# A decoder trunk in split fp32 on one core: seams of its squared-ReLU layers rearranged

## The chip, the core and the metric

The kernel runs on one core of a Trainium2 chip. A core has five engines that work side by side and each run their own instructions in order: TensorE (PE: matmuls and transposes into PSUM), VectorE (DVE), ScalarE (ACT), GpSimd (POOL) and SyncE (SP), which here issues the DMAs. They meet through semaphores. The metric is the device time of one execution in microseconds (us); before the change it is 2891.88 us, the median of three runs (2891.14 to 2891.97).

## What is computed

The reference is a trunk of two layers over 1024 tokens of width 1024 in fp32. Each layer has three sub-layers, all of the form h + RMSNorm(f(RMSNorm(h))) with a gain on both norms: a token mixer, a cross-attention into 256 memory tokens, and a squared-ReLU MLP. The mixer of layer 0 is a matrix-memory and recurrent block, that of layer 1 a sliding-window attention with rotary positions.

```python
def rms_norm(x, g):
    xf = x.astype(jnp.float32)
    y = xf * lax.rsqrt(jnp.mean(xf * xf, axis=-1, keepdims=True) + EPS)
    return (y * g.astype(jnp.float32)).astype(x.dtype)

def squared_relu_mlp(u, w1, w2):          # w1: 1024 x 4096, w2: 4096 x 1024
    return jnp.square(jax.nn.relu(u @ w1)) @ w2

    for l in range(DEPTH):                # DEPTH = 2
        u = rms_norm(h, g_mix_pre[l])
        # layer 0: mlstm_rglru_mixer(u, ...), layer 1: sliding_window_sink_attention(u, ...)
        h = h + rms_norm(u, g_mix_post[l])
        u = memory_cross_attention(rms_norm(h, g_x_pre[l]), mem, g_mem[l], w_xq[l], w_xkv[l], w_xo[l])
        h = h + rms_norm(u, g_x_post[l])
        u = squared_relu_mlp(rms_norm(h, g_ff_pre[l]), w_ff1[l], w_ff2[l])
        h = h + rms_norm(u, g_ff_post[l])
```

## The kernel before

Every fp32 operand of a product is split into a high and a low part (names ending in `h` and `l`: `split`, ScalarE copies the high part, VectorE subtracts for the low one), and a product is three matmuls of 128 x 128 by 128 x 512 on TensorE (`mm3`). Tokens are worked on in eight tiles of 128; tiles 0 to 3 and 4 to 7 are the two halves. A row of h stands in SBUF tiles of 128 x 1024, two column halves of 512.

The MLP is computed by the Strassen-Winograd scheme, seven products in place of eight, for both of its matrix products. In the first product the column blocks of `w1` run in 16 steps (the loop `for i in range(NP)`, with products p1 to p7 in each) and the squared result goes to DRAM (`hid`). In the second product the sum over 4096 runs in four chunks c, and each chunk has seven products in the order of the table `order`: p = 1, 2, 6, 5, 3, 7, 4. I call one of these 28 products a job; a job has four tiles of 128 tokens, each of 12 matmuls. Its left operand (`sh`) is loaded from `hid` in two halves `ar` by `lefts` and split; its right operand comes from four 1 MB blocks `b` of `w2` per chunk (`load_block`, `block_of`). The results stand in PSUM tiles `pa` and `pb` and are summed up by VectorE into the `acc` tiles (`gather`, and `tt`, an elementwise add or subtract). The pair 2 goes on in the PSUM tiles of 1, 3 in those of 5, 4 in those of 7. Where a bank `pb` is asked for, three tiles come from one PSUM pool (`G`) and the fourth from another (`T`), which also gives the tiles of the transposes (`tr`) and of the squares (`junk`).

After the last chunk comes the post-norm with the residual: `post(t)` for each tile adds the `u` part, squares it (ScalarE, with a sum along the row), multiplies it by the gain (GpSimd, `post_half`), takes the inverse root of the sum (`rsqrt`, a start value and three Newton steps on 128 x 1 numbers, nine small VectorE instructions), loads h, multiplies and adds (`post_norm`), and stores. In layer 0 the next mixer's pre-norm follows for the first four tiles (`pre_norm`): squares, root, `un` = h times root, then transposes on TensorE, which VectorE multiplies by the gain (`ut`) and ScalarE and GpSimd split into `uh` and `ul` (`transposed`). For the MLP's input the second half of the tokens goes through `transposed_sum`, which also forms Winograd's sums of the two halves.

The order of each engine's instructions is set by the code: `defer(delay, fn)` puts a piece of work into a queue that is emptied as a modelled clock of TensorE (`pe(us)`) passes its due time. `UD` is the delay from `un` to the transposes for the MLP's input, `MD` that for the next mixer's input, `N1` that from the squares to the root. `ready(u)` runs the queue until all tiles of an operand are there. TensorE's order is exactly the order of the code; the Tile framework orders the others.

## Time and profile before

| what | value |
|---|---|
| median of three runs | 2891.88 us |
| profiled execution | 2894.48 us |
| its span, first to last instruction | 2892.7 us |
| TensorE busy | 2686.7 us (93%) |
| VectorE busy | 2047.8 us (71%) |
| ScalarE busy | 1387.8 us (48%) |
| GpSimd busy | 546.9 us (19%) |
| mean granted clock of TensorE | 0.960 of full speed |

The times of all engines lie beside each other, so only the busy share of the fullest one says how near the program is to its bound; what an engine waited for, and where, is told by the list of waits and by the timeline. In them each row names the line of the kernel, the operation, its output and inputs, and in brackets the idle time before it with what ended that idle time. An `x` number says how many like instructions a row joins.

### The profile page before, as it was taken

How to read it: one execution, taken by the hardware profiler on the slowest of the kernel's cores; microseconds unless marked ns; L12 is line 12 of the kernel's file. 1: busy time of each engine (PE TensorE's matmuls, PEld its weight loads, DVE VectorE, ACT ScalarE, POOL GpSimd, SP SyncE). 2: the span in 40 equal slices, each digit the busy share in tenths (PEclk: the TensorE clock that was granted, in tenths of full speed). 3: DMA queues.
4: the chain of work that ended last, by engine and by line, in shares of the span. 5: the costliest groups of instructions: out<-in, count | busy, mean ns of one | idle time of the engine just before them, and what ended most of it. 6: DMA issues, size and time to landing. Idle time of an engine off the chain costs nothing. (4 is left out here: it accounts for less than half of the span.)

```text
span 2892.7 us, 35705 instructions
## 1 busy us (share of the span) xinstructions
PE 2686.7 (93%) x12846; PEld 2221.4 (77%) x12846; DVE 2047.8 (71%) x3604; ACT 1387.8 (48%) x2535; POOL 546.9 (19%) x434
## 2 busy tenths in 40 slices
PE   8999999999979999899987889879997999989996
PEld 8878778778867888788865668757886888878885
DVE  7776586656767666667786985785676766666778
ACT  5555545436544544443343773663544544444332
POOL 1351243442120000000023451560212000000003
PEclk9999999899999999999988989989998999999998
DMA  8633542225413444744334154023442344474433
GB/s 253 195 91 99 177 139 77 84 95 167 154 70 130 145 148 153 273 156 145 122 110 138 37 182 153 23 73 113 162 141 91 121 156 142 146 282 147 153 117 117
DMA packets 297314, 395.97 MB, mean 137 GB/s; under 512 B 16712, under 2 KB 172848, under 8 KB 297136
## 3 DMA queue, kind: packets, MB, share of 16 engines
q1 hardware_dynamic: 297136, 393.68, 41.2%
q8 instruction: 101, 1.65, 0.2%
q14 instruction: 77, 0.63, 0.1%
HBM read 297.15 MB, written 96.47 MB: 136 GB/s over the span
## 5 line engine op out<-in xcount | busy, mean ns | idle before, releaser
L230 DVE TENSOR_TENSOR w<-wr,w 128x1024 fp32r<-128x1024 f32 x248 | 321.0, 1297 | 208.8 <-ACT w L229 207.8
L83 PE MATMUL g<-uh,w 128*128 128x512 f32 x1152 | 378.5, 399 | 0.0
L83 PE MATMUL pa<-t,sh 128*128 128x512 f32 x1536 | 356.1, 392 | 17.4 <-ACT sh L229 16.8
L83 PEld LDWEIGHTS pa<-t,sh 128*128 128x128 f32 x1536 | 290.8, 190 | 80.1 <-ACT sh L229 17.7
L229 ACT ACTIVATE w<-wr 128x1024 fp32r<-128x1024 f32 x248 | 261.2, 1055 | 102.8 <-DMA wr<-in_w_xkv 26.6
L385 POOL TENSOR_TENSOR acc<-acc,gain 128x512 f32<-128x512 f32 x32 | 44.7, 1417 | 1262.0 <-DMA gain<-in_g_ff_post 1188.3
L83 PE MATMUL pb<-t,sh 128*128 128x512 f32 x1152 | 266.5, 392 | 3.0 <-DVE acc L767 3.0
L83 PEld LDWEIGHTS pb<-t,sh 128*128 128x128 f32 x1152 | 217.8, 189 | 48.8 <-DVE acc L767 3.5
L83 PEld LDWEIGHTS g<-uh,w 128*128 128x128 f32 x1152 | 217.2, 189 | 49.4
L229 ACT ACTIVATE t<-b 128x2048 fp32r<-128x2048 f32 x56 | 107.5, 1923 | 299.8 <-PE pa L83 164.5
L83 PE MATMUL g<-ul,w 128*128 128x512 f32 x576 | 228.4, 396 | 1.5 <-POOL ul L321 1.5
L230 DVE TENSOR_TENSOR sh<-ar,sh 128x1024 fp32r<-128x1024 f32 x112 | 136.8, 1234 | 100.7 <-PE pa L83 51.6
L83 PE MATMUL b<-t,w 128*128 128x512 f32 x768 | 180.0, 390 | 0.0
L321 POOL TENSOR_TENSOR ul<-ut,uh 128x512 fp32r<-128x512 f32 x80 | 114.2, 1449 | 345.8 <-ACT uh L320 345.8
L83 PE MATMUL g<-w,uh 128*128 128x512 f32 (+1 forms) x640 | 172.2, 359 | 3.4 <-ACT g L1464 3.4
L83 PE MATMUL b<-uh,wa 128*128 128x512 f32 x512 | 171.7, 396 | 1.5 <-ACT pc L847 1.5
L83 PEld LDWEIGHTS b<-t,w 128*128 128x128 f32 x768 | 144.2, 188 | 31.1
L83 PE MATMUL g<-w,pTh 128*128 128x512 f32 x512 | 160.1, 394 | 0.5 <-ACT pTh L229 0.5
L230 DVE TENSOR_TENSOR t<-b,t 128x2048 fp32r<-128x2048 f32 x56 | 127.8, 2285 | 2.1 <-ACT t L229 2.1
L83 PEld LDWEIGHTS g<-ul,w 128*128 128x128 f32 x576 | 108.8, 189 | 25.1 <-POOL ul L321 1.8
L83 PEld LDWEIGHTS g<-w,uh 128*128 128x128 f32 x640 | 110.1, 191 | 18.1 <-ACT g L1464 3.8
L83 PEld LDWEIGHTS b<-uh,wa 128*128 128x128 f32 x512 | 96.2, 188 | 25.4 <-ACT pc L847 2.3
(391 smaller groups left out, 5923.6 us busy)
## 6 DMA issues: line engine op xcount, KB each, us to landing
ar<-hid SPq DMA_DIRECT2D x112, 512.0 KB, 4.0
h<-h SPq DMA_DIRECT2D x100, 512.0 KB, 3.6
b<-in_w_ff SPq DMA_DIRECT2D x36, 1024.0 KB, 5.1
wr<-in_w_ff SPq DMA_DIRECT2D x64, 512.0 KB, 3.9
hid<-s SPq DMA_DIRECT2D x128, 256.0 KB, 2.3
wr<-in_ev_w_in SPq DMA_DIRECT2D x48, 512.0 KB, 3.8
hid<-c SPq DMA_DIRECT2D x94, 256.0 KB, 2.0
wr<-in_w_xkv SPq DMA_DIRECT2D x32, 512.0 KB, 5.9
```

The costliest lines, as they stand in the source:

```text
L83: ins = nc.tensor.matmul(*ar, **kw)
L229: act(out=h, in_=src, func=AF.Copy)
L230: (eng or vec).tensor_tensor(out=l, in0=src, in1=f(h), op=ALU.subtract)
L321: pool.tensor_tensor(out=ul[:, q], in0=t, in1=f(uh[:, q]), op=ALU.subtract)
L385: eng.tensor_tensor(out=dst, in0=y, in1=g[:, c], op=ALU.mult)
```

## The change

Four things are altered.

First, the transposes of the MLP's second input half are put off by `UL` = 7 units of the modelled clock after `un`, where it was `UD` = 14; those of the next mixer's first half by `MD` = 11, where it was 13.

Second, `lefts` is cut into the loads (`lefts_raw`) and the splits. Job 0's left operand takes both of its halves from the pool `wr`, and job 1's is loaded right behind it, before p6 of the last step of the first product.

Third, the post-norm of the MLP's output is spread over the last chunk. The gain is loaded in job p = 2, and the square and gain of a finished column half are done there (`weigh`), in p = 3, 7 and 4; the `u` part is added to 12, 22 and 21 in p = 6. Roots, residual and store are made for two tiles at once (`post_pair`, `rsqrt2`), at four places in p = 7 and p = 4. For tiles 0 to 3 of layer 0 `post_pair` also makes the next pre-norm up to `un`, which is written over the `acc` tiles.

Fourth, `left` is a set of tiles, and the sliding-window mixer waits for each tile of its operand where it uses it.

```diff
 RATIO = (0.0, 0.0)
-UD, MD = 14.0, 13.0
+UD, UL, MD = 14.0, 7.0, 11.0
 SD, SG = 14.5, 9.5
...
+    def rsqrt2(ss, n):
+        v = small(8, n)
+        x, xh, y, t = v[:, 0:2], v[:, 2:4], v[:, 4:6], v[:, 6:8]
+        vec.scalar_tensor_tensor(out=x, in0=ss[:, :, 0], scalar=D * EPS, in1=ss[:, :, 1], op0=ALU.add, op1=ALU.add)
+        vec.tensor_scalar(
+            out=y.bitcast(I32), in0=x.bitcast(I32), scalar1=-0.5, scalar2=float(0x5F3759DF + (5 << 23)), op0=ALU.mult, op1=ALU.add
+        )
+        vec.tensor_scalar(out=xh, in0=x, scalar1=-0.5 / D, scalar2=None, op0=ALU.mult)
+        for _ in range(3):
+            vec.tensor_tensor(out=t, in0=y, in1=y, op=ALU.mult)
+            vec.tensor_tensor(out=t, in0=t, in1=xh, op=ALU.mult)
+            vec.scalar_tensor_tensor(out=y, in0=t, scalar=1.5, in1=y, op0=ALU.add, op1=ALU.mult)
+        return y
     def gain(ap, in_w=False):
...
                 transposed_sum(un, g, u, first, c)
-            left[id(u)] -= 1
+            left[id(u)].discard(t)
...
         u = (U(n="uh", key=key), U(n="ul", key=key))
-        left[id(u)] = TPH
+        left[id(u)] = set(range(TPH))
         return u
-    def ready(u):
+    def ready(u, t=None):
-        while left[id(u)]:
+        while left[id(u)] if t is None else t in left[id(u)]:
             clock[0] = max(clock[0], pend[0][0])
...
-        def lefts(c, x):
-            h, lo = (wp.tile([P, 4, HALF], F32R, tag="w", name=nm("sh"), bufs=NW) for _ in range(2))
+        def lefts_raw(c, x, home="wh"):
+            rs = []
             for j in range(2):
-                if j == 0:
+                if home[j] == "w":
                     r = wp.tile([P, 2, HALF], F32, tag="wr", name=nm("ar"), bufs=NWR)
...
                 nc.sync.dma_start(out=r, in_=hid[x, r0 : r0 + 2 * P, :].rearrange("(i q) t -> q i t", q=P))
+                rs.append(r)
+            return rs
+        def lefts(rs):
+            h, lo = (wp.tile([P, 4, HALF], F32R, tag="w", name=nm("sh"), bufs=NW) for _ in range(2))
+            for j, r in enumerate(rs):
                 split(h[:, 2 * j : 2 * j + 2], lo[:, 2 * j : 2 * j + 2], r)
...
             if i == NP - 1:
-                left = lefts(0, 0)
+                left = lefts(lefts_raw(0, 0, "ww"))
+                next_raw = lefts_raw(0, 1)
             p6(i)
...
-        def post(t):
...
+        def weigh(key, t):
+            g, n = 4 * (key in ("21", "22")) + t, int(key in ("12", "22"))
+            post_half(acc[key, t], acc[key, t], late["g"], late["sy"][:, 2 * g : 2 * g + 2], n, pool)
+        def post_pair(t0):
+            keys = ("11", "12") if t0 < 4 else ("21", "22")
+            r = rsqrt2(late["sy"][:, 2 * t0 : 2 * t0 + 4].rearrange("p (t n) -> p t n", t=2), "rs")
+            hs = []
+            for j in range(2):
+                t = t0 + j
+                h = load_h(hsrc, t)
+                for n in range(2):
+                    cols = slice(n * HALF, (n + 1) * HALF)
+                    vec.scalar_tensor_tensor(
+                        out=h[:, cols], in0=acc[keys[n], t % 4], scalar=r[:, j : j + 1], in1=h[:, cols], op0=ALU.mult, op1=ALU.add
+                    )
+                    if after is None:
+                        nc.sync.dma_start(out=hdst[t * P : (t + 1) * P, cols], in_=h[:, cols])
+                if after is not None:
+                    nc.sync.dma_start(out=hdst[t * P : (t + 1) * P, :], in_=h)
+                hs.append(h)
+            if after is not None and t0 < 4:
+                ss = small(4, "ss")
+                for j in range(2):
+                    for n in range(2):
+                        square_sum(hs[j][:, n * HALF : (n + 1) * HALF], ss[:, 2 * j + n : 2 * j + n + 1])
+                r = rsqrt2(ss.rearrange("p (t n) -> p t n", t=2), "rs")
+                for j in range(2):
+                    un = [acc[k, t0 + j] for k in keys]
+                    act(out=un[0], in_=hs[j][:, 0:HALF], func=AF.Copy, scale=r[:, j : j + 1])
+                    vec.tensor_scalar(out=un[1], in0=hs[j][:, HALF:D], scalar1=r[:, j : j + 1], scalar2=None, op0=ALU.mult)
+                    after(t0 + j, un)
...
                     rt = block_of(*jobs[n + 1][:2])
-                    left = lefts(jobs[n + 1][0], jobs[n + 1][2])
+                    left = lefts(next_raw if n == 0 else lefts_raw(jobs[n + 1][0], jobs[n + 1][2]))
+                if c == 3 and p == 2:
+                    if t == 0:
+                        late["g"] = gain(a["g_ff_post"][l], True)
+                        late["sy"] = small(16, "sy", 1)
+                    weigh("11", t)
+                if c == 3 and p == 6:
+                    for k2 in ("12", "22", "21"):
+                        tt(acc[k2, t], acc[k2, t], acc["u", t], add)
+                if c == 3 and p == 3:
+                    weigh("12", t)
                 if last and p == 7:
...
                         xpool[0] = "xt"
-                        late["g"] = gain(a["g_ff_post"][l], True)
-                        late["sy"] = small(16, "sy", 1)
-                    else:
-                        post(t - 1)
-                elif last:
-                    post(3 if t == 0 else t + 3)
+                        post_pair(0)
+                    elif t == 1:
+                        post_pair(2)
+                if last:
+                    weigh(key, t)
+                    if p == 4 and t % 2 == 1:
+                        post_pair(t + 3)
             if c < 3:
...
                     load_block(c + 1, 3, 2)
-        post(7)
         if after is None:
...
         for t in range(TPH):
+            ready(u, t)
             ps = proj_tok(ws, u, t)
...
         un = {}
-        ready(uA)
+        if l == 0:
+            ready(uA)
         wpool[0] = WP[l]
...
                 in_steps(rope_tables(), 3, 3.5)
-            cross(l, half, ux[half], hm, hxr, lambda t, h, u=u, first=uf[0] if half else None: pre_norm(h, gf, u, t, UD, "x", first), None if half else mid)
+            cross(l, half, ux[half], hm, hxr, lambda t, h, u=u, first=uf[0] if half else None: pre_norm(h, gf, u, t, UL if first else UD, "x", first), None if half else mid)
         if stop == 2 + 3 * l:
...
                     un["a"] = new_u()
-                if t < TPH:
-                    pre_norm(h, gn, un["a"], t, MD)
+                u = un["a"]
+                c = slice(t * P, (t + 1) * P)
+                def rest():
+                    transposed(h, [(gn, u[0][:, :, c], u[1][:, :, c])])
+                    left[id(u)].discard(t)
+                defer(MD, rest)
```

Three places show how this moves instructions. The first is TensorE at the input of layer 0's MLP, where `tr` are transposes, `b` products of the MLP's first steps, `un_8168` (before) and `un_8189` (after) halves of tile 7's `un`. Before:

```order
2629 L83 MATMUL b_8187<-ul_5578,wa_8182 128x512
2630 L83 MATMUL b_8187<-uh_5577,wa_8182 128x512
2631 L87 MATMUL tr_8200<-cst,un_8035 128x128 x4
2632 L87 MATMUL tr_8207<-cst,un_8036 128x128 x4
2633 L87 MATMUL tr_8221<-cst,un_8112 128x128 x4
2634 L87 MATMUL tr_8228<-cst,un_8113 128x128 x4
2635 L87 MATMUL tr_8242<-cst,un_8168 128x128 x4
2636 L87 MATMUL tr_8249<-cst,un_8169 128x128 x4
2637 L83 MATMUL b_8292<-uh_7058,w_8268 128x512
```

After:

```order
2628 L87 MATMUL tr_8212<-cst,un_8112 128x128 x4
2629 L87 MATMUL tr_8219<-cst,un_8113 128x128 x4
2630 L83 MATMUL b_8208<-uh_5577,wa_8203 128x512
2631 L83 MATMUL b_8208<-ul_5578,wa_8203 128x512
2632 L83 MATMUL b_8208<-uh_5577,wa_8203 128x512 x2
2633 L83 MATMUL b_8208<-ul_5578,wa_8203 128x512
2634 L83 MATMUL b_8208<-uh_5577,wa_8203 128x512 x2
2635 L83 MATMUL b_8208<-ul_5578,wa_8203 128x512
2636 L83 MATMUL b_8208<-uh_5577,wa_8203 128x512
2637 L87 MATMUL tr_8242<-cst,un_8189 128x128 x4
2638 L87 MATMUL tr_8249<-cst,un_8190 128x128 x4
2639 L83 MATMUL b_8292<-uh_7058,w_8268 128x512
```

Before, six of the eight groups of four transposes stand together; now the last tile's two groups are alone, and the four others stand further ahead.

The second is the queue of SP where the MLP's second product begins. Of the loads `ar` before, 10656 is the second half of job 1's left operand and 10728 that of job 2's, and 10798 the first half of job 3's. Before:

```order
413 L980 DMA ar_10798<-hid 128x2x512
414 L838 DMA hid<-c_10535 128x512
415 L965 DMA b_10608<-in_w_ff 128x4x512
416 L965 DMA b_10610<-in_w_ff 128x4x512
417 L965 DMA b_10611<-in_w_ff 128x4x512
418 L965 DMA b_10609<-in_w_ff 128x4x512
419 L838 DMA hid<-c_10554 128x512
420 L838 DMA hid<-s_10620 128x512
421 L838 DMA hid<-s_10619 128x512 x2
422 L838 DMA hid<-s_10620 128x512
423 L980 DMA ar_10656<-hid 128x2x512
424 L980 DMA ar_10728<-hid 128x2x512
```

After, where 10570 is the second half of job 1's left operand, 10722 and 10796 are the first halves of jobs 2 and 3, and 10724 the second half of job 2's:

```order
410 L995 DMA ar_10570<-hid 128x2x512
411 L1008 DMA b_10520<-in_w_ff 128x4x512
412 L853 DMA hid<-c_10517 128x512
413 L995 DMA ar_10722<-hid 128x2x512
414 L995 DMA ar_10796<-hid 128x2x512
...
418 L980 DMA b_10613<-in_w_ff 128x4x512
419 L853 DMA hid<-c_10554 128x512
420 L853 DMA hid<-s_10624 128x512
421 L853 DMA hid<-c_10535 128x512
422 L853 DMA hid<-s_10623 128x512 x2
423 L853 DMA hid<-s_10624 128x512
424 L995 DMA ar_10724<-hid 128x2x512
```

Job 1's second half now stands before the four loads of `b`, job 2's still behind them.

The third is TensorE at the end of layer 0's MLP, where `pb` are tiles of p = 4 and `g` those of the mixer's projection. Before:

```order
5008 L83 MATMUL pb_12470<-t_12485,sh_12488 128x512
5009 L83 MATMUL pb_12470<-t_12484,sh_12489 128x512
5010 L87 MATMUL tr_12864<-cst,un_12633 128x128 x4
5011 L87 MATMUL tr_12873<-cst,un_12633 128x128 x4
5012 L87 MATMUL tr_12882<-cst,un_12686 128x128 x4
5013 L87 MATMUL tr_12891<-cst,un_12686 128x128 x4
5014 L87 MATMUL tr_12900<-cst,un_12735 128x128 x4
5015 L87 MATMUL tr_12909<-cst,un_12735 128x128 x4
5016 L87 MATMUL tr_12918<-cst,un_12784 128x128 x4
5017 L87 MATMUL tr_12927<-cst,un_12784 128x128 x4
5018 L83 MATMUL g_12964<-w_12946,uh_12543 128x512 x2
```

After:

```order
4978 L83 MATMUL pb_12507<-t_12523,sh_12532 128x512
4979 L87 MATMUL tr_12714<-cst,acc_10714 128x128 x4
4980 L87 MATMUL tr_12723<-cst,acc_10938 128x128 x4
4981 L87 MATMUL tr_12732<-cst,acc_10744 128x128 x4
4982 L87 MATMUL tr_12741<-cst,acc_10966 128x128 x4
4983 L83 MATMUL pb_12507<-t_12523,sh_12531 128x512
4984 L83 MATMUL pb_12507<-t_12524,sh_12531 128x512
4985 L83 MATMUL pb_12507<-t_12523,sh_12532 128x512
4986 L87 MATMUL tr_12753<-cst,acc_10758 128x128 x4
4987 L87 MATMUL tr_12762<-cst,acc_10980 128x128 x4
4988 L87 MATMUL tr_12771<-cst,acc_10772 128x128 x4
4989 L87 MATMUL tr_12780<-cst,acc_10994 128x128 x4
```

Before, the eight groups of transposes follow the last matmul of p = 4; now they stand within its second tile, and its last matmul is followed by the projection's first.

## Rows read from the trace of the kernel before

**Rows 1.** The page, engines: busy us (share of the span), instructions.

```profile
PE 2686.7 (93%) x12846; PEld 2221.4 (77%) x12846; DVE 2047.8 (71%) x3604; ACT 1387.8 (48%) x2535; POOL 546.9 (19%) x434
```

**Rows 2.** List of TensorE's waits: us in total, times, longest us.

```profile
PE b L83 <- ACT uh L344: 26.6, 2, 13.3
...
PE tr L87 <- DVE ut L317: 19.0, 4, 15.4
PE pa L83 <- ACT sh L229: 16.8, 2, 8.7
PE tr L87 <- ACT un L304: 11.6, 4, 8.0
```

**Rows 3.** Windows: per engine busy us (instructions), granted clock, DMA share, GB/s.

```profile
1150.00:1200.00 50.00, 46.66 (x204) 37.83 (x202) 33.15 (x35) 24.92 (x32) 0.00 (x0) 0.99 0.69 243
...
1500.00:1550.00 50.00, 17.17 (x59) 13.25 (x60) 40.54 (x108) 18.62 (x41) 19.03 (x15) 0.56 0.59 200
1550.00:1600.00 50.00, 49.23 (x244) 40.30 (x243) 30.31 (x75) 21.47 (x56) 17.66 (x23) 1.00 0.23 72
```

**Rows 4.** Timeline of TensorE at A: start, us, instruction [idle before <-releaser].

```profile
848.38 1.91 PE L87 MATMUL tr<-cst,un 128*128 128x128 f32 x16
...
866.37 0.79 PE L83 MATMUL b<-uh,w 128*128 128x512 f32 x1 [13.30 <-ACT uh L344]
```

**Rows 5.** Timeline of VectorE at A.

```profile
865.23 0.68 DVE L767 TENSOR_TENSOR wr<-wr,wr 128x512 f32<-128x512 f32 x1
865.83 2.29 DVE L230 TENSOR_TENSOR w<-wr,w 128x1024 fp32r<-128x1024 f32 x1
```

**Rows 6.** Timeline of TensorE at B.

```profile
1204.82 1.22 PE L83 MATMUL pa<-t,sh 128*128 128x512 f32 x2 [8.16 <-ACT sh L229]
```

**Rows 7.** Timelines of ScalarE and of SP's queue at B.

```profile
1203.71 1.06 ACT L229 ACTIVATE sh<-ar 128x1024 fp32r<-128x1024 f32 x1 [1.29 <-DMA ar<-hid]
...
1184.25 2.72 SPq L965 DMA_DIRECT2D b<-in_w_ff  x4
...
1192.99 10.22 SPq L980 DMA_DIRECT2D ar<-hid  x5
```

**Rows 8.** Timeline of TensorE at C.

```profile
1477.97 19.20 PE L83 MATMUL pb<-t,sh 128*128 128x512 f32 x84
1500.21 5.49 PE L83 MATMUL pb<-t,sh 128*128 128x512 f32 x12 [3.05 <-DVE acc L767]
1512.59 1.97 PE L87 MATMUL tr<-cst,un 128*128 128x128 f32 x8 [6.89 <-ACT junk L295]
...
1543.63 2.79 PE L87 MATMUL tr<-cst,un 128*128 128x128 f32 x12 [15.37 <-DVE ut L317]
1546.08 1.14 PE L83 MATMUL g<-w,uh 128*128 128x512 f32 x2
```

**Rows 9.** Timeline of VectorE at C.

```profile
1513.64 1.11 DVE L284 SCALAR_TENSOR_TENSOR rs<-rs 128x1 f32<-128x1 f32 x1
...
1528.08 0.22 DVE L284 SCALAR_TENSOR_TENSOR rs<-rs 128x1 f32<-128x1 f32 x1
...
1535.46 0.48 DVE L305 TENSOR_SCALAR un<-h,rs 128x512 f32<-128x512 f32 x1
1539.27 1.42 DVE L393 SCALAR_TENSOR_TENSOR h<-acc,rs,h 128x512 f32<-128x512 f32 x2 [3.33 <-DMA h<-h]
```

**Rows 10.** Timeline of GpSimd at C.

```profile
1510.78 7.62 POOL L385 TENSOR_TENSOR acc<-acc,gain 128x512 f32<-128x512 f32 x6 [6.11 <-ACT junk L295]
```

**Rows 11.** Timelines of TensorE, GpSimd, VectorE and SP at D.

```profile
2845.78 21.92 PE L83 MATMUL pb<-t,sh 128*128 128x512 f32 x96
...
2882.67 2.77 POOL L385 TENSOR_TENSOR acc<-acc,gain 128x512 f32<-128x512 f32 x2 [4.53 <-ACT junk L295]
...
2888.34 1.41 DVE L393 SCALAR_TENSOR_TENSOR h<-acc,rs,h 128x512 f32<-128x512 f32 x2
...
2889.12 0.99 SPq L395 DMA_DIRECT2D out<-h  x2
```

More of the change, by code (lines that the diff above doesn't have):

```diff
@@ L1080, in mlp @@
         late = {}
-        def post(t):
-            keys = ("11", "12") if t < 4 else ("21", "22")
-            ss = late["sy"][:, 2 * t : 2 * t + 2]
-            y = [acc[key, t % 4] for key in keys]
-            for n in range(2):
-                if keys[n] != "11":
-                    tt(y[n], y[n], acc["u", t % 4], add)
-                post_half(y[n], y[n], late["g"], ss, n, pool)
-            h = post_norm(y, ss, hsrc, hdst, t)
-            if after is not None:
-                after(t, h)
+        def weigh(key, t):
[29 more added lines that the diff above has]
+                    after(t0 + j, un)
         for n, (c, p, x, bank, more, key) in enumerate(jobs):
```

## The prediction

> **What bounds the kernel now.** I read the page's shares first: TensorE is busy 2686.7 of 2892.7 us [rows 1], so the program is bound by TensorE and the change can only win or lose what lies in its 206 us of idle time and in its clock. The list of waits of TensorE comes next, because it says whose delay that idle time is [rows 2]. The reader is to see there that the largest waits are few and long: two of 13.3 us for the sum's high part (`uh`), two of up to 8.7 us for a left operand (`sh`), one of 15.4 us for the gain product (`ut`), some of up to 8.0 us for `un`. The timeline then puts each at a place. I call them A (the input of the MLP, in both layers, near 866 us in layer 0), B (the MLP's second product starts, near 1204 us in layer 0), C (from the first MLP to the attention, 1500 to 1546 us) and D (the end, after TensorE's last matmul). B and C stand out in the windows too: a granted clock of 0.56 of full speed in 1500 to 1550 us against 1.00 just after, and a DMA share of 0.69 in 1150 to 1200 us [rows 3]. Of the two levels of the clock (1.2 and 2.4 GHz) C lies mostly at the lower one, after TensorE had stood still.
>
> **A, the shorter delay (UL = 7 instead of 14).** Before, the transposes of the half's tiles 1, 2 and 3 follow each other, and only then DVE gets its work on them: the first matmul of the next product waits 13.30 us for `uh` [rows 4]. From 851.7 to that matmul DVE runs some 26 instructions that mostly follow each other 0.60 us apart, 18 of them the six per tile of these three tiles; the split of a weight took 2.29 us [rows 5]. In the changed order the transposes of tile 0 lie in the output projection before, those of tiles 1 and 2 among the `b` matmuls, and only tile 3's are last. Its six instructions and nine others, about 15, stay behind the last `un`: (26 - 15) x 0.60 = 6.6 us earlier. The 11 that move enter a stretch in which DVE is already full, so the last `un` is pushed: I take 1.1 us off and keep 5.5. Ends: 3 us if half of it is pushed back; 8 us if only tile 3's own chain (six times 0.60 and a copy on ScalarE, some 5 us) is left of the 13.3. The transposes that now stand earlier cost TensorE nothing more: as many as before, 0.12 us each [rows 4]. Two layers: **11 us**, from 6 to 16.
>
> **B, the left operand loaded first.** The first product has done 54 matmuls and then waits 8.16 us for ScalarE's copy `sh` [rows 6]. That copy ends a wait for a DMA: the second half of job 1's left operand is issued by SP in the group that starts at 1192.99, behind four loads of 1 MB issued from 1184.25, and the copy starts at 1203.71 [rows 7]. The change issues both halves for jobs 0 and 1 before those four loads, and neither needs a buffer that becomes free late: job 0 takes two of the three `wr` slots, job 1 one of them and one `h` slot. The wait of 8.16 us goes, and its twin of 8.7 us in layer 1 [rows 2]. What is late next is job 2's left operand, the second half of which still stands behind the four loads in SP's queue; job 2 starts some 22 us after job 0, at 1206 without the wait, and its half then has 13 us from its issue at 1193, where job 1's was there 10.7 us after the group's start [rows 7]. So I take 0.4 us off each: **16 us** for both. Ends: 10 us, if job 2 is 3.5 us late in each layer because the DVE rows for its block stand ahead of its split; 18 us with the two matmuls at the lower clock behind the wait.
>
> **C, the post-norm spread over the last chunk.** Before, TensorE ends the last product at 1505.7, does 32 transposes in pieces with idle times of 6.89, 8.03 and 15.37 us before them, and the first projection matmul stands at 1546.08 [rows 2, 8]. The work it waits for is DVE's, tile by tile: last `un` at 1535.46, then tiles of which `h` is loaded late (3.33 us) [rows 9], though the projection needs only the first four tiles. The change moves twelve adds ahead (no more than before), does the roots of two tiles in 12 small instructions instead of 2 x 9 (108 to 72 in this layer), puts the last four tiles' post-norm behind the first four's transposes, and lets the projection wait tile by tile. All eight groups of transposes now stand in p4's second tile. Without any wait the last two products would end at 1499.8 (12 matmuls are 2.7 us [rows 8]), with 32 transposes of 0.12 us at 1503.6. That is the far end: 1546.1 - 1503.6 = 42 us won. I do not take it, because new waits appear. The fourth tile of p7 takes a PSUM slot that the square of `h` of tile 2 has held, and that square follows the whole root of the pair: by DVE's rows I put it at 1497 instead of 1486, an 11 us wait that was not there. Then p7 ends at 1499.7, 15 matmuls more at 1505; the transposes wait for squares and `un` until about 1510 and for `ut` some 1.5 us more; 3.8 us of transposes and 30 matmuls (6.8 us) end near 1522. With 2 us for the first heads' transposes behind the projection the gain is 1546 - 1522 - 2 = **22 us**. The near end is 8 us: the chain of `un` as late as before, 1535.5, and the projection directly after it. DVE's backlog of some 10 us is paid in the next stretch, where DVE is busy 30 of 50 us [rows 3].
>
> Here VectorE and GpSimd work side by side: a root step of line 284 took 1.11 us while six multiplies ran on GpSimd, and 0.22 after GpSimd's last one [rows 9, 10]. The Trainium skill, "SBUF — State Buffer", section "Who interferes with whom", says that the two engines share a port pair under an exclusive lock, which a VectorE instruction with two SBUF inputs takes part in; the rows agree, since line 284 reads two. By that rule 10 of the 12 instructions of a paired root can each stand behind a whole multiply; by rows I count two such waits per pair, 2.5 us, and this is in the 1497 above.
>
> **D, the end.** TensorE's last matmul ends at 2867.7, DVE's last row stands at 2888.34, the last store is issued at 2889.12 and the span ends at 2892.7 [rows 11]. DVE is simply behind: four tiles' post-norm is left. Now the adds and three of the four pairs are earlier. After the last matmul the last pair's own chain remains: gather and square, 2 us (an estimate from 0.68 for a DVE row of this size [rows 5], twice, and the hand-over); from the last tile's multiplies at 2882.67 to the end of `h` before took 7.1 us, and two more `h` rows of 0.7 make 8.5 to 9; the store 3.6: 2867.7 + 2 + 9 + 3.6 = 2882.3, with 1.4 us (half of the 3.05 before p4's last tile [rows 8]) for a wait of TensorE in p4: **9 us**. Ends: 4, if the pair before is still in work; 13, if nothing is.
>
> **The sum.** 11 + 16 + 22 + 9 = 58 us off the profiled execution, 2894.5 (its span of 2892.7 and 1.8 around it): 2836.5. The median of the runs, 2891.9, is 2.6 below that execution, so **2834**. Its own range, 2824 to 2846.
>
> **Rivals.**
> - *C's new wait eats C.* If TensorE waits for each pair's root in p7 and p4, and not once, the products end where the transposes did before: C is 2 and the time 2854. For it: the small instructions stretched fivefold beside GpSimd. Against it: 36 fewer of them, and tiles 4 to 7 out of the way.
> - *Nothing new waits.* C gives 40 and D 13: 2812. For it: DVE is idle half of the first products of the chunk. Against it: the slot of the square.
> - *B is a matter of bandwidth, not of order*, so the change does not do what it says: with a DMA share of 0.69 the wait moves from job 1 to job 2 in full, B is 0 and the time 2850. Against it: the transfers of the group at 1192.99 took 10 us, and 22 us are there.
> - *Slower.* p4 goes on in the PSUM tiles of p7, so each of its tiles first needs DVE's sum of the one before it, and DVE works in order. If each sum stands behind a whole pair's post-norm (12 root steps of 0.22 [rows 9] with 2.5 us beside GpSimd, four `h` rows, where there is a next layer a second root and two `un`: 11 us, of which a tile hides 2.7), TensorE loses 8 us at each of four pairs, 64 us in two layers: 2898. It decides from the seventh of the eight pairs (58 us won, 8 each). For it: the wait of 3.05 us for `acc` before p4's last tile is one of this kind [rows 8]. Against it: the order on DVE sets the sums between a pair's pieces, and only two of the eight pairs have a second root.
>
> **Chances.** Forecast 0.50, C eaten 0.18, nothing new waits 0.13, B by bandwidth 0.12, slower 0.04, and 0.03 for no change that can be told. The range of 8 in 10 reaches to all faster cases: 2808 to 2862. Faster by over 0.2% (5.8 us, about what these runs can tell from no change): 0.94; within it 0.02; slower 0.04.
>
> **What would show it.** A: the wait for `uh` before the first matmul of p2 is under 10 us. B: no wait for `sh` in the first two jobs; if one over 3 us stands before job 2, the third rival. C: one wait of some 11 us in p7's fourth tile, the first projection matmul near 1509 us (1546 less A's and B's 13.5 of layer 0 and 24 of C); the granted clock above 0.8 in the stretch. D: less than 17 us from TensorE's last matmul to the span's end. The forecast is wrong if TensorE waits at more than two tiles of p7 and p4, or if A's wait stays at 13 us.

## The result and the profile after

The changed kernel takes 2844.2 us (median of four runs, 2842.4 to 2848.7), the kernel before 2891.9 beside it: a ratio of 0.9836 with an interval of 0.9819 to 0.9853. It is 1.6% faster. The profiled execution took 2842.4 us with a span of 2840.6, so its span is 52.1 us shorter than that of before.

Since TensorE's order is fixed by the code, the same matmul can be looked up in two traces, and the difference of its start says what was won up to there. The table gives what each stage added to this difference (negative: won), in us, between these marks: A ends with the first `ts` matmul behind p2, B with the first tile of the fourth job, C with the first transposes of the queries, D is what lies between TensorE's last matmul and the span's end. "A, layer 1" holds layer 1's mixer too. The two kernels of the experiments that change nothing there (e2, e3) moved by +1.8 and +2.4 in it, so it is not good to less than that. B is no finer: with the same edit it reads from -6.6 to -8.8 in layer 0 and from -6.9 to -9.4 in layer 1. C reads from -22.1 to -22.6 in the kernels that have its edits and no other there, and -0.4 and -1.6 in the two that have none; D agrees to 0.2 us.

```
              A l0   B l0     C    A l1   B l1     D    span
after         -1.5   -8.8  -22.4   -1.8   -9.3   -8.7  2840.6
e1_delay      -1.5   +1.6   -0.4   -2.3   +0.4    0.0  2890.3
e2_left       -0.6   -7.2   -1.6   +1.8   -9.0   -0.1  2876.0
e3_post       -0.1   +1.0  -22.1   +2.4   +1.0   -8.6  2866.6
e4_sums       +1.0   -8.7  -22.5   -1.3   -6.9   -8.7  2845.8
e5_utact      -3.4   -8.7  -22.6   -4.7   -9.4   -8.7  2835.5
e6_late       -2.0   -8.7  -22.3   -1.1   -9.4   -8.8  2840.8
e7_junk       -1.3   -8.6  -22.3   -2.4   -9.0   -8.7  2840.7
e8_junklate   -2.0   -6.6  -21.7   -1.4   -7.6   -8.7  2845.1
e9_quad       -1.8   -8.5  -25.0   -0.8   -7.4   -8.7  2840.8
e10_best      -2.4   -8.7  -25.3   -5.5   -7.3   -8.8  2835.0
e11_roots     -1.9   -8.7  -21.7   -0.9   -7.4   -7.9  2844.2
e12_sumspool  +2.1   -7.2  -22.1   +6.6   -7.3   -8.7  2856.4
```

The list of TensorE's waits in the changed kernel (us in total, times, longest) answers to [rows 2]. The waits for `sh` in the first jobs and the long one for `ut` are gone. The two waits of 13.3 us for `uh` at A have not gone, they have become 10.5 us (layer 0) and 11.0 us (layer 1) for `w`.

```profile
PE b L83 <- ACT w L229: 21.5, 2, 11.0
...
PE pb L83 <- ACT junk L310: 8.5, 1, 8.5
PE tr L87 <- ACT junk L310: 6.3, 2, 4.8
PE tr L87 <- ACT un L319: 5.0, 2, 2.5
...
PE pb L83 <- ACT sh L229: 2.7, 2, 1.4
```

TensorE's timeline of the changed kernel at A, where the first matmul of p2 stood at 866.37 [rows 4], with VectorE's and ScalarE's rows below it:

```profile
854.43 1.53 PE L87 MATMUL tr<-cst,un 128*128 128x128 f32 x8 [2.50 <-ACT un L319]
866.50 0.79 PE L83 MATMUL b<-uh,w 128*128 128x512 f32 x1 [10.54 <-ACT w L229]
```

```profile
853.92 0.48 DVE L320 TENSOR_SCALAR un<-h,rs 128x512 f32<-128x512 f32 x1
...
864.68 0.68 DVE L782 TENSOR_TENSOR wr<-s,wr 128x512 f32<-128x512 f32 x1
```

```profile
865.39 1.06 ACT L229 ACTIVATE w<-wr 128x1024 fp32r<-128x1024 f32 x1
```

VectorE's rows of the kernel before, and TensorE's second matmul of p2 there:

```profile
851.27 0.48 DVE L305 TENSOR_SCALAR un<-h,rs 128x512 f32<-128x512 f32 x1
...
864.02 0.68 DVE L767 TENSOR_TENSOR wr<-s,wr 128x512 f32<-128x512 f32 x1
```

```profile
868.78 0.79 PE L83 MATMUL b<-ul,w 128*128 128x512 f32 x1 [1.62 <-DVE ul L345]
```

The last `un` comes 2.65 us later. The copy `w` takes the results of the second and third of the weight block's four sums, and the third (`wr<-s,wr`) starts at 864.68 where it stood at 864.02. So `w` is 0.7 us later, and the matmul stands where it stood. The 1.5 us that the table has for A come behind it: the second matmul waited 1.62 us for `ul` before, and does not wait now. At B, where TensorE waited 8.16 us [rows 6], the first two jobs now run without a break, and a short wait stands in the third:

```profile
1182.36 21.95 PE L83 MATMUL pa<-t,sh 128*128 128x512 f32 x96
1204.14 1.52 PE L83 MATMUL pb<-t,sh 128*128 128x512 f32 x6
1207.03 0.73 PE L83 MATMUL pb<-t,sh 128*128 128x512 f32 x2 [1.37 <-ACT sh L229]
1208.29 9.36 PE L83 MATMUL pb<-t,sh 128*128 128x512 f32 x40 [0.53 <-DVE sh L230]
```

At C, TensorE's timeline answers to [rows 8]. The reader is to see the new wait before p7's fourth tile, the transposes within p4, the projection at 1506.00 in place of 1546.08, and two waits for the projection's weights behind it:

```profile
1484.53 8.90 PE L83 MATMUL pb<-t,sh 128*128 128x512 f32 x27 [8.48 <-ACT junk L310]
1493.27 1.47 PE L87 MATMUL tr<-cst,acc 128*128 128x128 f32 x12
1496.24 0.66 PE L87 MATMUL tr<-cst,acc 128*128 128x128 f32 x4 [1.50 <-ACT junk L310]
...
1506.00 0.63 PE L83 MATMUL g<-w,uh 128*128 128x512 f32 x2
...
1512.17 0.49 PE L83 MATMUL g<-w,uh 128*128 128x512 f32 x1 [1.81 <-ACT w L229]
1516.40 0.79 PE L83 MATMUL g<-w,uh 128*128 128x512 f32 x1 [3.73 <-DVE w L230]
```

The windows answer to [rows 3]. The rate of the DMAs up to B is as before, and the granted clock around C is 0.90 and 0.93, where it was 0.56 from 1500 to 1550 us.

```profile
1150.00:1200.00 50.00, 50.00 (x220) 40.98 (x219) 33.25 (x35) 26.76 (x34) 0.00 (x0) 1.00 0.68 243
1460.00:1510.00 50.00, 40.01 (x181) 32.67 (x179) 42.84 (x94) 22.90 (x52) 23.85 (x18) 0.90 0.45 156
1510.00:1560.00 50.00, 44.46 (x205) 35.92 (x204) 36.69 (x88) 18.81 (x45) 14.81 (x19) 0.93 0.44 158
```

At D TensorE ends at 2824.3 (below), VectorE's last rows start at 2835, and the span ends 16.3 us behind TensorE, where it was 25.0 [rows 11].

```profile
2802.10 22.23 PE L83 MATMUL pb<-t,sh 128*128 128x512 f32 x96
...
2834.98 2.74 DVE L1119 SCALAR_TENSOR_TENSOR h<-acc,rs,h 128x512 f32<-128x512 f32 x4
```

### The profile page after: what moved, and what is told of

Same layout as the page of the kernel before. It is cut to its first block, busy times and chain, and to the rows that moved or that the text cites. A ratio compares the mean times of both kernels' runs of the same rounds, so it can differ in the third digit from the quotient of the medians.

```text
span 2840.6 us, 35656 instructions
## 1 busy us (share of the span) xinstructions
PE 2678.9 (94%) x12846; PEld 2214.3 (78%) x12846; DVE 2043.0 (72%) x3544; ACT 1384.7 (49%) x2535; POOL 535.7 (19%) x434
```

## Experiments

**The parts alone.** e1_delay is the kernel before with the one edit of the delay:

```diff
-UD, MD = 14.0, 13.0
+UD, UL, MD = 14.0, 7.0, 13.0
-            cross(..., pre_norm(h, gf, u, t, UD, "x", first), ...)
+            cross(..., pre_norm(h, gf, u, t, UL if first else UD, "x", first), ...)
```

> The kernel before with the shorter delay alone (7 instead of 14 for the second half's transposes), in both layers. Read by the place of TensorE's matmuls against the kernel before. Theory 1: VectorE is full from the last but one root to the first matmul of p2, so moving transposes only changes the order of the same VectorE work, and w (the sums of the weight blocks, then ScalarE's copy) is late at the same time: 1.5 us earlier per layer, 3 in all (2889). Rival (the prediction's term A): 11 us (2881) when nothing else of the change stands beside it.

It took 0.9994 of the time before (0.9985 to 1.0004). The first matmul of p2 stands at 866.52 and waits 10.38 us for `w`. The table has -1.5 and -2.3 at A. Theory 1's numbers came there, and the prediction's term A did not: 11 us would be a ratio of 0.9962, outside the interval. By the runs' times alone theory 1's 3 us can't be told from nothing.

e2_left is the kernel before with `lefts_raw` and its two early calls, as in the change's diff and nothing else.

> The kernel before with the left operand of jobs 0 and 1 loaded first, alone. Theory: order of the queue; the wait of 8.16 us in layer 0 and of 8.68 in layer 1 go and a wait of about 1.9 us before job 2 takes its place, 17 to 18 us off: 2874. Rival: bandwidth; the same bytes are loaded at a DMA share near 0.7, job 2 waits what job 1 no longer does, 0 to 5 us off: 2887 to 2892.

0.9936 (0.9921 to 0.9950), 16.7 us by the span, of which 7.2 and 9.0 at B. Order it is: the loads are the same, and their rate from 1150 to 1200 us is 243 GB/s at a DMA share of 0.69, as before [rows 3]. Job 2 now waits 1.89 us in both layers, where job 1 waited 8.58 and 8.68. What job 2 waits may be bandwidth: the share is 1.00 in the changed kernel from 1182 to 1204 us.

e3_post is the changed kernel with the other two parts taken back:

```diff
-                left = lefts(lefts_raw(0, 0, "ww"))
-                next_raw = lefts_raw(0, 1)
+                left = lefts(lefts_raw(0, 0))
-                    left = lefts(next_raw if n == 0 else lefts_raw(jobs[n + 1][0], jobs[n + 1][2]))
+                    left = lefts(lefts_raw(jobs[n + 1][0], jobs[n + 1][2]))
-            cross(..., UL if first else UD, ...)
+            cross(..., UD, ...)
```

> The changed kernel with the delay of 14 back and job 1's left operand loaded as before: the spread post-norm, the roots of two tiles and the wait per tile are left. Theory: the seams do not touch each other; 22 us at the end of layer 0's MLP and 9 at the end of the kernel, 31 us off: 2861. Rival: the spread post-norm gains only because the work before it comes earlier or later than it would, as less of the DMA and VectorE load collides: 20 us or less off, 2872 or more.

0.9888 (0.9872 to 0.9904), with -22.1 at C and -8.6 at D. As far as the table can tell, the seams do not touch each other; the three spans' gains, 2.4 + 16.7 + 26.1, come to 45.2 of the 52.1, the rest being stages without an edit that drift by 1 to 2 us. By the ratios of the runs the parts (0.06%, 0.64%, 1.12%) come to 1.82%, above the 1.64% of the whole, so the sum agrees to 5 to 7 us either way.

**What holds A.** e4_sums is the changed kernel with two calls moved:

```diff
+        prep_sums(0)
+        prep_23(0)
         p1(1)
         ready(u[1])
-        prep_sums(0)
-        prep_23(0)
```

> The changed kernel with the sums and the split of the first weight block (w of p2) placed before p1's second step, ahead of the wait for the second half's tiles. Theory 1 (VectorE has no free time at this seam): the wait for w goes, but the instructions that are moved ahead of the tile's sums make uh late in its place; the first matmul of p2 stands where it stood, within 1 us, or up to 2 us later. Rival (only w's place in the order is late): the wait for w of 10.5 us falls by 2 us or more in each layer, 4 to 6 us off the changed kernel.

0.9835 (0.9819 to 0.9851). TensorE's first matmul of p2 waits for `uh` again, and stands 2.8 us later than in the changed kernel, a little more than the 2 us that were allowed; VectorE's rows before it show why, since the split of the weight now stands between the tile's own instructions:

```profile
869.32 0.80 PE L83 MATMUL b<-uh,w 128*128 128x512 f32 x1 [12.88 <-ACT uh L359]
```

```profile
858.57 2.30 DVE L230 TENSOR_TENSOR w<-wr,w 128x1024 fp32r<-128x1024 f32 x1
...
867.20 0.68 DVE L358 TENSOR_TENSOR ut<-ut,uh 128x512 f32<-128x512 f32 x1
```

e5_utact takes work from VectorE in place of moving it:

```diff
+            if n == 0:
                 vec.tensor_tensor(out=t, in0=ps..., in1=g[:, q, None]..., op=ALU.mult)
+            else:
+                for k in range(4):
+                    act(out=t[:, k], in_=ps[:, k * P : (k + 1) * P], func=AF.Copy, scale=g[:, 4 + k : 5 + k])
```

> The changed kernel with the gain product of the upper four blocks (ut, one of two per tile in the sum of the halves) made by four small ScalarE instructions in place of one of VectorE. Theory 1 (VectorE's work sets the first matmul of p2): four VectorE instructions of 0.60 us less, so p2 starts 1.5 to 2.5 us earlier in each layer, 3 to 5 us off the changed kernel. Rival (a chain from the last tile's un to uh sets it, not the sum of the work): ScalarE's four small instructions are slower than one of VectorE's and lie in that chain; no gain, or 1 us slower per layer.

0.9827 (0.9809 to 0.9846). The matmul comes 2.2 us earlier than in the changed kernel, and A is -3.4 against -1.5 in layer 0 (-4.7 against -1.8 in layer 1). Four instructions of 0.60 us were taken away. A is not good to such a difference alone: e10_best, with the same edit, has -2.4 and -5.5. Firmer is the time from the start of the last tile's transposes to that of the matmul. It is 12.1 us in the changed kernel and in e1_delay (854.43 to 866.50 and 854.45 to 866.52) and 10.5 us in e5_utact and e10_best (853.86 to 864.34 and 855.00 to 865.50), 1.6 us less. Theory 1 stands, though the medians (2841.7 and 2844.2) and intervals do not tell the two kernels apart.

```profile
864.34 0.80 PE L83 MATMUL b<-uh,w 128*128 128x512 f32 x1 [9.39 <-ACT uh L363]
```

e12_sumspool is e4_sums with the four sums on GpSimd:

```diff
-            tt(s1, a21, a22, add)
-            tt(a21, a11, a21, sub)
-            tt(a11, s1, a11, sub)
-            tt(a12, a12, a11, sub)
+            for o, x, y, op in ((s1, a21, a22, add), (a21, a11, a21, sub), (a11, s1, a11, sub), (a12, a12, a11, sub)):
+                (pool if i == 0 else vec).tensor_tensor(out=o, in0=x, in1=y, op=op)
```

> As the run with the first weight block's sums placed ahead, but those four sums on GpSimd in place of VectorE. If VectorE's work alone counts, 2.4 us per layer earlier than that run. If each GpSimd instruction holds up one VectorE instruction for about 1.1 us, as in the rows of before (1.83 in place of 0.68), VectorE loses 4.4 us for the 2.4 saved and p2 starts at the same time as in that run or up to 2 us later.

0.9852 (0.9836 to 0.9868). VectorE has four instructions less and the matmul comes 1.8 us later than in e4_sums, at 871.15. GpSimd's rows and VectorE's of the same stretch show the price: beside each of the four sums one VectorE instruction takes about 1.1 us more (alone line 285 takes 0.15, line 284 0.22, line 360 0.68, line 320 0.48). The last `un` (line 320) and so the last transposes come later by it. The profiled execution was the slowest of the four, 2858.2 us where the others took 2849 to 2850, so its stages behind A in layer 0 are not read.

```profile
851.77 1.71 POOL L815 TENSOR_TENSOR s<-wr,wr 128x512 f32<-128x512 f32 x1
853.56 1.66 POOL L815 TENSOR_TENSOR wr<-wr 128x512 f32<-128x512 f32 x1
855.30 1.27 POOL L815 TENSOR_TENSOR wr<-s,wr 128x512 f32<-128x512 f32 x1
856.65 1.60 POOL L815 TENSOR_TENSOR wr<-wr,wr 128x512 f32<-128x512 f32 x1
```

```profile
852.28 1.21 DVE L285 SCALAR_TENSOR_TENSOR rs<-rs 128x1 f32<-128x1 f32 x1
...
854.02 1.22 DVE L284 SCALAR_TENSOR_TENSOR rs<-rs 128x1 f32<-128x1 f32 x1
...
855.35 1.77 DVE L360 TENSOR_TENSOR ul<-ut,uh 128x512 fp32r<-128x512 f32 x1
857.05 1.49 DVE L320 TENSOR_SCALAR un<-h,rs 128x512 f32<-128x512 f32 x1
```

**What holds C.** Theory 2 is that two waits of TensorE follow each other here, the one for the PSUM slot and those for `w` behind it, so that either alone is worth little. e7_junk gives the squares of `h` another place:

```diff
-                        square_sum(hs[j][:, n * HALF : (n + 1) * HALF], ss[:, 2 * j + n : 2 * j + n + 1])
+                        act(out=acc["u", t0 + j], in_=hs[j][:, n * HALF : (n + 1) * HALF], func=AF.Square, accum_out=ss[:, 2 * j + n : 2 * j + n + 1])
```

> The changed kernel with the squares of h in the next layer's pre-norm written to SBUF (the acc tiles of u, which are free by then) and not to PSUM. The prediction's step: p7's fourth tile waits 8.48 us for a PSUM slot that such a square holds. If so the wait goes. Theory 2 says that little of it is won, since the projection then stands earlier and waits for w at the same time, 1511 to 1516 us: the wait for w grows from 5.5 to 9 us or more, 0 to 2 us off the changed kernel. Rival: the slot's wait is on the path that sets the end, 8 us off.

0.9833 (0.9816 to 0.9850). The wait of 8.48 us is gone, so it was the PSUM slot; C is -22.3 as before (-22.4). In its place the transposes wait 14.3 us for squares, roots and `un`, where the changed kernel has 1.5:

```profile
1484.20 1.09 PE L87 MATMUL tr<-cst,acc 128*128 128x128 f32 x8 [1.76 <-ACT acc L1135]
1490.05 1.12 PE L87 MATMUL tr<-cst,acc 128*128 128x128 f32 x4 [4.75 <-ACT junk L310]
1491.61 1.12 PE L87 MATMUL tr<-cst,acc 128*128 128x128 f32 x4 [0.44 <-ACT junk L310]
1492.38 1.53 PE L83 MATMUL pb<-t,sh 128*128 128x512 f32 x3
1501.21 3.68 PE L87 MATMUL tr<-cst,acc 128*128 128x128 f32 x16 [7.31 <-ACT acc L1135]
```

So the slot's wait alone is worth nothing, but theory 2's series of slot and `w` is only half right: the waits for `w` went to 0.78 us, and what grew is the wait for `un`. This is not a chain that stood ready behind the slot. The second pair's `un` (ScalarE's row, first of the changed kernel, then of e7_junk) comes 10 us later:

```profile
1490.09 1.34 ACT L1135 ACTIVATE acc<-h,rs 128x512 f32<-128x512 f32 x2 [3.06 <-DVE rs L300]
```

```profile
1500.44 1.33 ACT L1135 ACTIVATE acc<-h,rs 128x512 f32<-128x512 f32 x2 [2.50 <-DVE rs L300]
```

Its root takes 4.2 us of VectorE's time line in the changed kernel (1485.83 to 1490.0) and 10.4 us here (1489.94 to 1500.35), as a split of a weight and four gain products of the first pair stand between its steps. The waits from p7's fourth tile to the first keys' transposes add up to 15.5 us in the changed kernel and 15.0 here, and the keys stand at 1527.93 and 1528.02. The edit changed the order of VectorE's work and not its end. That VectorE's work as a whole sets C (it is busy 42.8 of the 50 us from 1460) fits this, but no run takes more than a few small instructions from it here.

e6_late moves the last two pairs of layer 0 in the code, and e8_junklate does both edits:

```diff
-                    if p == 4 and t % 2 == 1:
+                    if p == 4 and t % 2 == 1 and after is None:
                         post_pair(t + 3)
+                    elif p == 4 and t == 3:
+                        post_pair(4)
+                        post_pair(6)
```

> The changed kernel, in layer 0 with the post-norm of tiles 4 to 7 put behind the last matmul of the last product, in place of between its tiles. Theory 2: the projection's waits for w (1.81 and 3.73 us) come from VectorE's sum of p4's third tile standing behind the roots of tiles 4 and 5, with ScalarE's square and the copy of w behind that; they go, 5 to 7 us off the changed kernel. Rival: VectorE has the same work to do before the keys' transposes and the waits come back there, 0 to 2 us.

> Both: squares of h to SBUF, and tiles 4 to 7 behind the last matmul. Theory 2 (slot and w in series): more than either alone, 8 to 11 us off the changed kernel. Rival: no more than the later post-norm alone.

e6_late, 0.9848 (0.9829 to 0.9866), gave nothing (C -22.3) and told nothing: VectorE's order did not follow the place in the code, and p4's third sum stands in the middle of the same roots as in the changed kernel.

```profile
1504.64 1.22 DVE L293 TENSOR_SCALAR rs<-rs 128x2 int32<-128x2 int32 x1
...
1509.25 0.69 DVE L782 TENSOR_TENSOR acc<-pb,acc 128x512 f32<-128x512 f32 x1
```

e8_junklate, 0.9837 (0.9822 to 0.9851), then is e7_junk with other noise (C -21.7), and the 8 to 11 us expected of it were wrong.

e9_quad forces the order by a dependence: one root for four tiles, which needs the last tile's square.

```diff
-    def rsqrt2(ss, n):
-        v = small(8, n)
+    def rsqrt2(ss, n, m=2):
+        v = small(4 * m, n)
...
-                    if p == 4 and t % 2 == 1:
+                    if p == 4 and t % 2 == 1 and after is None:
                         post_pair(t + 3)
+                    elif p == 4 and t == 3:
+                        post_pair(4, 4)
```

> The changed kernel, in layer 0 with one root for all of tiles 4 to 7, after the last product: since it needs the last tile's square, it can't be scheduled between the sums of p4. The place of the earlier run's two pairs did not change VectorE's order; this one does. Theory 2: the projection's waits for w (1.8 and 3.7 us, and the lower clock behind them) come from the roots that stand between VectorE's sums of p4's tiles; they go, 5 to 8 us off the changed kernel. Rival: VectorE's work before the keys is the same, the waits come back at the keys' transposes, 0 to 2 us off.

0.9815 (0.9802 to 0.9829). The sums of p4 now stand ahead of the root, and the projection does not wait for `w` at all. At the first keys' transposes 4.5 us more than in the changed kernel are won (1523.40 against 1527.93); at the queries' 2.6 are left (-25.0 against -22.4). The new wait is for the keys, behind eight `h` rows on VectorE:

```profile
1523.40 0.66 PE L87 MATMUL t<-cst,ksh 128*128 128x128 f32 x4 [3.21 <-ACT ksh L1685]
```

```profile
1503.17 1.28 DVE L782 TENSOR_TENSOR acc<-pb,acc 128x512 f32<-128x512 f32 x2
...
1515.10 5.39 DVE L1119 SCALAR_TENSOR_TENSOR h<-acc,rs,h 128x512 f32<-128x512 f32 x8
```

That lies between theory 2 and its rival. The waits for `w` were the sums behind roots. Of what that gives, 3.2 us come back as the wait for the keys, and 1.9 more are lost behind it, where the granted clock is 0.79 from 1520 to 1528 us (0.97 in the changed kernel).

**The roots, and the best version.** e11_roots is the changed kernel with `rsqrt` for each tile in `post_pair`:

```diff
-            r = rsqrt2(late["sy"][...].rearrange("p (t n) -> p t n", t=2), "rs")
+            r = [rsqrt(late["sy"][:, 2 * t0 + 2 * j : 2 * t0 + 2 * j + 2], "rs") for j in range(2)]
...
```

> The changed kernel with a root for each tile (nine instructions each) in place of one for two (twelve). The prediction's count: 36 more small VectorE instructions in layer 0 and 24 in layer 1. If they lie on the chain, at 0.1 to 0.2 us each where two chains interleave, layer 0's seam is 2 to 4 us and the end 0.5 to 1.5 us later. Rival: the roots hide in waits for squares and multiplies; within 1 us of the changed kernel.

0.9828 (0.9815 to 0.9841). C is 0.7 us later than in the changed kernel, D 0.8 us; the wait for the slot is 9.85 us in place of 8.48. The two-tile roots are a small part of the gain, and the runs' times do not tell the two kernels apart.

e10_best is the edits of e5_utact and e9_quad together.

> The changed kernel with the gain product of the upper blocks on ScalarE in the sum of the halves, and with one root for tiles 4 to 7 in layer 0. Theories 1 and 2 together: 4 us (2.2 in each layer, as measured alone) and what the single root gives, 5 to 8: 9 to 12 us off the changed kernel, 2832 to 2835. Rival: the two seams share nothing, but what is won at the end of the MLP is lost at the keys: 4 us off.

0.9805 (0.9792 to 0.9818), median 2838.1. By the spans it is 5.6 us below the changed kernel, by the medians 6.1, and by the ratios to the kernel before, which ran beside each, 9. Its interval lies just below that of the changed kernel (0.9819 to 0.9853), so it is the fastest here, but how much it gains on the changed kernel is open. The single root gives less than expected, as in e9_quad.

## Why the prediction was right, and where it was not

The forecast was 2834 us, the measurement 2844: 48 us won of 58. Point by point by the spans:

- **B**, forecast 16: 18 (8.8 and 9.3). The wait went, and job 2 is late next, as the step said, by 1.9 us in each layer where I had 0.4. That error is covered by another, the clock: behind the wait it was 0.82 from 1204 to 1218 us, and in the changed kernel it is 1.00, behind a wait too (the rows below, before and after). Job 1 had taken 21.7 us in layer 0, 8.6 of it waits and 10.9 what an undisturbed job takes, so the lower clock cost 2.2; job 2 now takes 13.4, of which the clock is 0.6. That is luck too: in e2_left, behind the same wait in layer 0, the clock was 0.89 from 1204 to 1220 us and job 2 took 15.0. e2_left excludes the rival of bandwidth for all but job 2's wait.

```profile
1204.00:1218.00 14.00, 12.76 (x48) 9.98 (x49) 6.92 (x6) 5.86 (x7) 0.00 (x0) 0.82 0.85 323
```

```profile
1204.00:1218.00 14.00, 12.11 (x53) 9.39 (x52) 11.17 (x10) 6.73 (x7) 0.00 (x0) 1.00 0.98 366
```

- **C**, forecast 22: 22.4. Its new wait stands where it was put, at p7's fourth tile, with 8.48 us for 11. But that wait alone is worth nothing (e7_junk): without it TensorE waits as long for `un`. What I had put as 2 us between the projection's start and the heads' transposes was 7.4, 5.5 of it waits for `w`. The projection itself started 29.8 us earlier, less A and B, where I had 24. The size was right by luck, by two errors that cancel. TensorE's only wait at a tile of p7 and p4 is this one of 8.48 us, which answers the rivals that C is eaten, that nothing new waits, and that the change is slower.
- **D**, forecast 9: 8.7, from TensorE's end to the span's end 16.3 us.
- **A**, forecast 11: 3.2. This is the step that failed: "(26 - 15) x 0.60 = 6.6 us earlier". The count was wrong: VectorE's rows between the last `un` and the matmul are 22 before, not 26, and 16 after, twelve of the last two tiles and four of the weight's sums. From that `un` to the matmul it was 15.1 us and is 12.6, so 2.5 us are won and not 6.6. What moved ahead was let to cost 1.1 us; VectorE was busy 9.8 of the 10 us from 840 us there, and the `un` was pushed 2.65. That leaves nothing, and 1.5 us in layer 0 come from the wait for `ul` behind the matmul, which the prediction did not name. I also did not ask what else p2's first matmul needs: it waits for `w` now, 0.7 us later than before. e1_delay, e4_sums and e5_utact show it from three sides: moving work on a full engine changes the name of the wait, taking four instructions away shortens it by 1.6 us or more.
- **The sum.** A's miss is 7.8 us, and B's is 2.0 the other way: 52.1 in place of 58 by the profiled executions. The rest of the distance between the medians comes from my taking off 2.6 us, by which before's profiled execution lay above its median; that of the changed kernel lies 1.8 below its own.

Of the signs in the prediction, A's wait under 10 us failed (the wait for `uh` is gone, but 10.5 us for `w` stand there), and the rest held: no `sh` wait in the first two jobs, a clock of 0.90 at C, less than 17 us at D. The wait for each tile in the mixer (`ready(u, t)`) could not matter: all eight groups of transposes stand ahead of the projection in TensorE's order, so that nothing was left to wait for. It was not run alone.

The rule that was weighed held in kind, and the price that was taken for it was high: of the 120 instructions of the ten paired roots 17 were held up, by 15.6 us in all, 1.6 us per root in place of 2.5. The Trainium skill, "SBUF — State Buffer", section "Who interferes with whom", counts among the instructions that contend with GpSimd not only those with two SBUF inputs but also one-input forms in a two-port mode. e12_sumspool agrees with the first (1.21 us for 0.15 and 1.22 for 0.22). The second I had overlooked; line 320, with one input of 512 columns, agrees with it (1.49 us for 0.48), and it is in the section below.

## What to carry to other kernels

Where an engine has no gap before a wait, as VectorE at A, an edit that moves its work earlier can leave the wait where it is, under another operand's name. Count what the waiting instruction needs in all, and the engine's work up to there, from the rows, before crediting a new order. A wait that is seen is that of the latest of several operands: take it away alone (e7_junk) before it is priced. A load that stood behind four big ones in a queue was worth its wait here, 8.6 us in each layer less the 1.9 that the next job waits.

## What was not expected of the hardware

The paired root's two instructions with one input were held up beside GpSimd, those of the single root never were. The lists of one line's durations in ns (min/median/max) show it, first of the kernel before (128x1), then of the changed one (128x2), and last of e11_roots, where single roots stand in the places of the paired ones:

```profile
L279 DVE TENSOR_SCALAR rs<-rs x98: 138/152/156, 15.8 to 2885.4; 128x1 int32<-128x1 int32 x98
```

```profile
L293 DVE TENSOR_SCALAR rs<-rs x10: 154/1069/1227, 1464.9 to 2832.0; 128x2 int32<-128x2 int32 x10
L296 DVE TENSOR_SCALAR rs<-rs x10: 154/156/1332, 1466.0 to 2833.0; 128x2 f32<-128x2 f32 x10
```

```profile
L279 DVE TENSOR_SCALAR rs<-rs x98: 135/150/157, 16.1 to 2837.1; 128x1 int32<-128x1 int32 x98
```

In e11_roots 17 of these 98 run while GpSimd is busy, and none takes over 0.16 us. Two elements in place of one thus cost up to 1.2 us more where GpSimd works, though alone they take the same 0.16; four elements (e9_quad) cost no more than two, 1.22 us beside GpSimd and 0.16 without. The Trainium skill, "VectorE: DVE Perf Modes", section "Mode 2×_2P — use both read ports for one tensor", says that this mode halves the outermost dimension that is longer than one between the two ports; a 128x1 operand has none to halve. That would explain it, but that the mode was taken here is inferred from the delays alone.
